# Expert stage of a two-layer decoder trunk: the tokens kept in float32, the gather's split, the slot lists and the register reads moved, and another ending

## The chip, the cores and the metric

The kernel runs on one core of one Trainium2 chip. The metric is the device time of one execution in microseconds (us); the number before the change is the median of three runs. One more execution was recorded by the hardware profiler, and all rows below come from that one. A piece of time under 0.2% (3.8 us) can't be told from no change here.

## What is computed

The reference is a trunk of two layers on 256 tokens of width 1024. Each layer mixes tokens (an attention and a linear attention beside each other), then channels. The change lies in the channel mixing of the second layer, a top-2-of-8 expert SwiGLU with a layer norm behind it:

```python
logits = (x @ router_w).astype(jnp.float32)
top_val, top_idx = lax.top_k(logits, TOP_K)
...
for e in range(N_EXPERTS):
    y = y + gates[..., e:e + 1] * swiglu(x, w_gate[e], w_up[e], w_down[e])
...
x = layer_norm(DN_ALPHA * x + f, ln2_g[layer], ln2_b[layer])
```

Gate and up are 1024 x 3584 per expert, down is 3584 x 1024, everything in float32.

## The kernel before

**Pieces and splits.** All weights come as pieces of 128 x 1024 floats (512 KB) through SP's queue, in one fixed list (`Stream`, L114 to 194): 84 pieces for an expert, 672 in all. A float32 product is made of reduced-precision matmuls: ScalarE rounds a piece to `whi` (L165), VectorE takes the rest `wlo = raw - whi` (L167), and TensorE multiplies the parts. `raw`, `whi` and `wlo` tiles, the gathered tokens and the split tokens all live in one pool of 36 equal slots, tag `k4`. A piece that is marked plain isn't split; TensorE multiplies it in float32, which it records as two matmuls. `caps(raw, spl)` says how many pieces are loaded ahead of the split and split ahead of use in the order in which the program is written: (14, 5) in the expert stage.

**Steps and chunks.** `moe` (L1593) takes the experts by `RANKS`, a sorting by load made on the chip: position 0 is expert 0, the others by rising rank number. Step i computes gate (`mg`) and up (`mu`) of position i in seven chunks of 512 columns, and in the same chunks the down product (`oe`) of position i-1. Even steps are "wide" experts (128 tokens; three matmuls for gate and up: L473 to L475); odd steps are "narrow" ones (64 tokens, both halves of their split tokens in one stationary tile; two matmuls: L1543 and L1544). Down is plain for wide experts (L1557) and split for narrow ones. So an even step has 16 x 3 + 16 matmuls per chunk, an odd one 16 x 2 and 8 float32 products. Step 0 has no down and starts with chunk 1, since `dense` computes expert 0's chunk 0 for all tokens while the router works. After step 7 the down product of the last narrow expert stands alone, first half f=0 of the columns, then f=1, seven chunks each. I call this the last product.

**Chains.** The rest runs in generators that are advanced once per matmul group (`tick`); `lag(n)` lets n ticks pass. `route` (L1259) computes the lists of tokens per expert; its last part is a row of small VectorE instructions that ends with `cnti` (L1360). `gather(i)` (L1375) collects the tokens of the next narrow and the next wide expert by multiplying the tokens with a 0/1 matrix `Pt`: eight blocks of four matmuls (L1394) whose stationary operands are `xnh` and `xnl`, the tokens split once in `route` (L1289 to L1294) and kept in four slots to the end. Gathers 1 to 4 start in chunk 2 of steps 0, 2, 4 and 6; gather 4 has no wide expert, so it takes two slots fewer than gathers 1 to 3. `slots(r)` (L1407) turns the list round: two transposes (L1420) and two products with the gates `gtr` (L1422). It is added at the head of each step. `hidden` and `hidden_t` compute silu(gate) * up and transpose it (L1467, L1481). `scatter` (L1493) multiplies the result of a finished expert (`oh`, `ol`) with the turned list and adds it to `x` (L1511).

**Order.** From behind `dense` on, TensorE, VectorE and ScalarE run as written (`as_written`). SP's loads stand in their list, each waiting for its slot. Expert numbers other than 0 are only known on the chip: SP reads them from `eidi` into registers (L437), at the place where the scheduler put it.

**End.** `overflow` (L1639) reads a count into registers and skips, by a branch (L1649), a loop that isn't needed when no expert has too many tokens. Then `ln_params` loads scale and shift of the last norm, 512 KB each (L1134), and `last_norm` (L1625) computes it.

Of the kernel before, what the change touches and what calls it, by code (L numbers as in the profile page):

```python
# [18 lines left out]
P = 128  # L19
# [94 lines left out]
class Stream:  # L114
# [24 lines left out]
    def dma_to(self, i):  # L139
        while self.n_dma <= min(i, len(self.subs) - 1):  # L140
            src, n, _ = self.subs[self.n_dma]
            if callable(src):
                src = src()
            t = self.k.k4([P, 2, 512], name="raw")
            self.k.nc.sync.dma_start(t[:, :, :n], src[:, :2 * n].rearrange("p (k n) -> p k n", k=2))
            self.raw[self.n_dma] = t
            self.n_dma += 1
# [40 lines left out]
class Kern:  # L188
# [234 lines left out]
    def plan(self):  # L423
# [18 lines left out]
        def add(nm, r, c, j):  # L442
            W.add((nm, r, c, j), [piece(r, i) for i in moe_pieces(nm, c, j)], 512, nm == "md" and self.plain(r))
# [12 lines left out]
    def plain(self, r):  # L456

        return r not in NARROW
# [800 lines left out]
    def route(self):  # L1259
# [20 lines left out]
        self.xn = [[], []]  # L1280
        for t in range(2):
# [7 lines left out]
            hi = self.k4([P, D], F32R, name="xnh")  # L1289
            lo = self.k4([P, D], F32R, name="xnl")  # L1290
            nc.scalar.copy(hi, self.x[t])
            nc.vector.tensor_tensor(lo, self.x[t], f32(hi), op=OP.subtract)
            self.xn[0].append(hi)
            self.xn[1].append(lo)  # L1294
# [80 lines left out]
    def gather(self, i):  # L1375
# [117 lines left out]
    def scatter(self, e, f, oe):  # L1493
# [8 lines left out]
        self.flags.add(("oh", e, f))  # L1502
        yield
# [11 lines left out]
    def down(self, r, c, fs=(0, 1)):  # L1515
# [77 lines left out]
    def moe(self):  # L1593
        nc = self.nc
        self.Pt, self.xe, self.PT, self.ht = {}, {}, {}, {}
        self.taken = False
        self.add_chain(self.route(), ("route",), 1)
        self.dense()
        first = len(self.traced())
        for i, r in enumerate(RANKS):  # L1600
            self.add_chain(self.slots(r), ("slots", r), 1)
            for c in range(0 if i else 1, 7):
                if i % 2 == 0 and c == 2 and i < NE - 1:
# [3 lines left out]
                res = {}  # L1607

# [5 lines left out]
                if i:  # L1614
                    self.run(self.down(RANKS[i - 1], c))
        for f in range(2):
# [5 lines left out]
        g2, b2 = self.ln_params(2, 1, nc.sync)  # L1622
        self.last_norm(g2, b2)

    def last_norm(self, g, b):  # L1625
        nc = self.nc
        mv = [self.norm_stats(t, LN_EPS) for t in range(2)]
        for t in range(2):
            x = self.x[t]
            nb = self.small([P, 1], "nb", 2)  # L1630
            nc.vector.scalar_tensor_tensor(nb, mv[t][:, 0:1], -1.0, mv[t][:, 3:4], op0=OP.mult, op1=OP.mult)
            for h in range(2):
                s = slice(h * 512, (h + 1) * 512)
                nc.scalar.activation(x[:, s], x[:, s], AF.Identity, bias=nb, scale=mv[t][:, 3:4])
                nc.vector.tensor_tensor(x[:, s], x[:, s], g[:, s], op=OP.mult)  # L1635
                (nc.vector if h else nc.gpsimd).tensor_tensor(x[:, s], x[:, s], b[:, s], op=OP.add)  # L1636
                nc.sync.dma_start(self.out[0, t * P:(t + 1) * P, s], x[:, s])

    def overflow(self):  # L1639
# [3 lines left out]
        n = nc.values_load(self.cnti[0:1, 0:1], min_val=0, max_val=S)  # L1643
# [5 lines left out]
        with tc.If(n > 0):  # L1649
            with tc.For_i(0, NE, 1) as e:  # L1650
# [16 lines left out]
                for d in range(8):  # L1667
                    ps = self.bg("xe")
                    for j in range(2):
                        for t in range(2):  # L1670
                            nc.tensor.matmul(ps[:, :P], lhsT=f32(self.xn[j][t])[:, d * P:(d + 1) * P], rhs=p2[:, t],
                                             start=(j == 0 and t == 0), stop=(j == 1 and t == 1))
# [44 lines left out]
    def build(self):  # L1717
# [9 lines left out]
        self.CAP_MOE = (14, 5)  # L1727
        self.LAG = 9
# [56 lines left out]
```

## Time and profile before

| | us |
|---|---|
| median of 3 runs (1896.32 to 1897.02) | 1896.44 |
| the profiled execution | 1896.58 |
| its span in the trace | 1894.8 |
| step 0 (expert 0, chunk 1) starts | 981.49 |
| steps 1, 2, 3 start | 1059.98, 1166.60, 1280.28 |
| steps 4, 5, 6, 7 start | 1392.26, 1504.90, 1616.96, 1729.32 |
| the last product starts and ends | 1837.76, 1875.03 |

The page gives TensorE as busy for 97% of the span, VectorE 77%, ScalarE 61%. Its slices show that the DMA engines are almost full from slice 21 on (about 995 us), which is the expert stage, and only 30% to 60% busy before. So the two halves of the program have different limits, and the shares of the whole span say little about either. A TensorE matmul of 512 columns shows a duration of 0.39 us, but the next one starts 0.23 us after it; starts, not durations, tell the pace.

### The profile page before, as it was taken

The page shows a single profiled execution, that of the slowest core. Times are in us where ns is not written, and L with a number is a line of the kernel's source. Part 1 is how long each engine was busy: PE and PEld are TensorE (multiplying, and loading weights), DVE is VectorE, ACT ScalarE, POOL GpSimd, SP SyncE. Part 2 cuts the span into 40 slices and gives each one's busy share as a digit, 9 for nine tenths or more (in the row PEclk, how much of TensorE's full clock was granted, in tenths as well). Part 3 has the DMA queues.
Part 4 walks back from the last instruction along what each step waited for, and adds up shares of the span by engine and source line. Part 5 has one row for each costly group of instructions (what it writes and reads, how often), then busy time and mean ns, then how long its engine had stood idle before and what let it go on. Part 6 is the DMA issues. An engine that isn't in the chain of part 4 may idle for free. (4 is left out here: it accounts for less than half of the span.)

```text
span 1894.8 us, 27869 instructions
## 1 busy us (share of the span) xinstructions
PE 1844.7 (97%) x9279; PEld 1466.0 (77%) x9279; DVE 1459.6 (77%) x2147; ACT 1164.2 (61%) x1710; POOL 163.0 (9%) x221
## 2 busy tenths in 40 slices
PE   8999999999999999999999999999999999999995
PEld 7998888888889998888878766886678766787663
DVE  7888666675556887757588878998788977989777
ACT  6664555454444754545357767786678866787673
POOL 2113202000001212201220000000000000000000
PEclk9999999999999999999999999999999999999997
DMA  9445343674655445444749999999999999999992
GB/s 322 140 147 179 134 150 115 203 242 147 196 200 191 142 137 189 135 147 145 252 159 335 384 409 408 366 395 391 410 400 365 402 394 409 396 372 409 409 409 107
DMA packets 154374, 513.50 MB, mean 271 GB/s; under 512 B 26320, under 2 KB 28592, under 8 KB 154224
## 3 DMA queue, kind: packets, MB, share of 16 engines
q1 hardware_dynamic: 151984, 504.10, 72.1%
q0 software_dynamic: 2240, 7.56, 1.2%
q8 instruction: 75, 1.23, 0.3%
q14 instruction: 75, 0.61, 0.1%
HBM read 506.09 MB, written 5.51 MB: 270 GB/s over the span
## 5 line engine op out<-in xcount | busy, mean ns | idle before, releaser
L167 DVE TENSOR_TENSOR wlo<-raw,whi 128x1024 fp32r<-128x1024 f32 (+1 forms) x838 | 997.3, 1215 | 219.2 <-ACT whi L165 175.2
L165 ACT CAST whi<-raw 128x1024 fp32r<-128x1024 f32 x838 | 849.7, 1047 | 238.0 <-PE oe L1557 63.6
L1557 PE MATMUL oe<-raw,htp 128*128 128x512 f32 x448 | 197.5, 592 | 0.0
L1557 PEld LDWEIGHTS oe<-raw,htp 128*128 128x128 f32 x448 | 84.7, 190 | 94.6 <-issue 91.9
L627 PE MATMUL qb<-xhl,whi 128*128 128x256 f32 x384 | 110.4, 288 | 0.0
L632 PE MATMUL qb<-xhl,wlo 128*128 128x256 f32 x384 | 108.9, 283 | 0.6 <-DVE wlo L167 0.6
L630 PE MATMUL qb<-xhl,whi 128*128 128x256 f32 x384 | 108.5, 283 | 0.0
L473 PE MATMUL at<-whi,xhl 128*128 128x512 f32 x256 | 106.8, 417 | 0.0
L475 PE MATMUL at<-whi,xhl 128*128 128x512 f32 x256 | 101.2, 395 | 0.0
L474 PE MATMUL at<-wlo,xhl 128*128 128x512 f32 x256 | 100.8, 394 | 0.0
L1543 PE MATMUL mg<-whi,xen 128*128 128x512 f32 x224 | 97.4, 435 | 0.0
L1115 POOL TENSOR_TENSOR bnmv<-bnmv,mhalf 128x1 f32<-128x1 f32 x8 | 7.0, 871 | 1006.6 <-DVE bnmv L1114 1006.6
L1543 PE MATMUL mu<-whi,xen 128*128 128x512 f32 x224 | 91.5, 409 | 0.0
L1544 PE MATMUL oe<-wlo,htn 128*128 128x512 f32 x224 | 89.6, 400 | 0.9 <-DVE wlo L167 0.9
L1543 PE MATMUL oe<-whi,htn 128*128 128x512 f32 x224 | 89.6, 400 | 0.0
L1544 PE MATMUL mu<-wlo,xen 128*128 128x512 f32 x224 | 88.7, 396 | 0.0
L1544 PE MATMUL mg<-wlo,xen 128*128 128x512 f32 x224 | 87.8, 392 | 0.0
L473 PE MATMUL mg<-whi,xe 128*128 128x512 f32 x216 | 87.7, 406 | 0.0
L475 PE MATMUL mg<-whi,xe 128*128 128x512 f32 x216 | 85.2, 394 | 0.0
L473 PE MATMUL mu<-whi,xe 128*128 128x512 f32 x216 | 85.1, 394 | 0.0
L474 PE MATMUL mg<-wlo,xe 128*128 128x512 f32 x216 | 84.9, 393 | 0.0
L475 PE MATMUL mu<-whi,xe 128*128 128x512 f32 x216 | 84.3, 390 | 0.0
(456 smaller groups left out, 3817.5 us busy)
## 6 DMA issues: line engine op xcount, KB each, us to landing
raw<-in_moe SPq DMA_DIRECT2D x672, 512.0 KB
raw<-in_trunk SPq DMA_DIRECT2D x270, 512.0 KB
lx<-LT SPq DMA_DIRECT2D x8, 256.0 KB
Dm<-dx SPq DMA_DIRECT2D x8, 256.0 KB
raw<-in_trunk SPq DMA_DIRECT2D x8, 256.0 KB
lng<-in_ln_g POOLq DMA_DIRECT2D x3, 512.0 KB, 5.8
lnb<-in_ln_b POOLq DMA_DIRECT2D x3, 512.0 KB, 8.0
dx<-zero POOLq DMA_DIRECT2D x4, 256.0 KB, 5.0
```

The costliest lines, as they stand in the source:

```text
L165: k.last_act = nc.scalar.copy(hi[:, :, :n], raw[:, :, :n])
L167: ins = (nc.gpsimd if share and a else nc.vector).tensor_tensor(lo[:, a:b, :n], r[:, :, :n], f32(hi)[:, a:b, :n], op=OP.subtract)
L473: nc.tensor.matmul(o, lhsT=xh, rhs=hi[:, kk, :n], start=st, stop=False)
L474: nc.tensor.matmul(o, lhsT=xh, rhs=lo[:, kk, :n], start=False, stop=False)
L475: mm = nc.tensor.matmul(o, lhsT=xl, rhs=hi[:, kk, :n], start=False, stop=en)
L627: nc.tensor.matmul(o, lhsT=hi[:, kk, w], rhs=self.xhl[k // 2][:, k % 2, :S], start=(k == 0 and b % 2 == 0), stop=False, skip_group_check=True)
L630: nc.tensor.matmul(o, lhsT=hi[:, kk, w], rhs=self.xhl[k // 2][:, k % 2, S:], start=False, stop=False, skip_group_check=True)
L632: self.dense_pe = nc.tensor.matmul(o, lhsT=lo[:, kk, w], rhs=self.xhl[k // 2][:, k % 2, :S], start=False, stop=(k == 7), skip_group_check= ...
L1115: nc.gpsimd.tensor_tensor(mv[:, 3:4], mv[:, 2:3], self.mhalf[:, 0:1], op=OP.pow)
L1543: nc.tensor.matmul(o, lhsT=x(k0 + kk), rhs=hi[:, kk], start=first and i == 0 and kk == 0, stop=False)
L1544: nc.tensor.matmul(o, lhsT=x(k0 + kk), rhs=lo[:, kk], start=False, stop=last and end)
L1557: nc.tensor.matmul(o, lhsT=x(k0 + kk), rhs=w[:, kk], start=first and i == 0 and kk == 0, stop=last and end)
```

## The change

- `route` no longer splits the tokens. It copies them in float32 into two slots `xs` (before: four slots), and each of the eight blocks of each gather splits its own 128 x 256 part into `xsh` (ScalarE) and `xsl` (VectorE) right before its matmuls. These small tiles use buffers of the layer's convolution.
- `slots(r)` is added in chunk 3 of a step and not in front of its first chunk.
- SP reads an expert's number behind the load that precedes its first use; the count for the branch, behind the last load.
- Scale and shift of the last norm are loaded before the expert stage as 4 x 256 rows, split in two parts, and spread over the partitions by eight matmuls at the end. `last_norm` takes its statistics for tokens 128 to 255 on ScalarE.
- In the last product f=1, chunks 3 to 6 are plain float32 pieces. `caps` is (8, 5) from chunk 6 of step 7 on and (6, 8) in the last product. The scatter of f=0 lags six ticks more.

```diff
             if callable(src):
-                src = src()
+                with self.k.behind(self.last_dma):
+                    src = src()
...
-    def plain(self, r):
-        return r not in NARROW
+    def plain(self, r, c=0, f=0):
+        return r not in NARROW or (r == RANKS[-1] and f == 1 and c > 2)
...
-        self.xn = [[], []]
+        self.xs = [self.k4([P, 2, 512], name="xs") for _ in range(2)]
...
-            hi = self.k4([P, D], F32R, name="xnh")
-            lo = self.k4([P, D], F32R, name="xnl")
-            nc.scalar.copy(hi, self.x[t])
-            nc.vector.tensor_tensor(lo, self.x[t], f32(hi), op=OP.subtract)
...
+            for h in range(2):
+                nc.scalar.copy(self.xs[h][:, t], self.x[t][:, h * 512:(h + 1) * 512])
...
         for d in range(8):
             yield from self.take()
+            x = self.xs[d // 4][:, :, d % 4 * P:(d % 4 + 1) * P]
+            xp = [self.mp.tile([P, S], F32R, name=nm, tag=tag, bufs=3).rearrange("p (t c) -> p t c", t=2)
+                  for nm, tag in (("xsh", "cth"), ("xsl", "cy"))]
+            nc.scalar.copy(xp[0], x)
+            nc.vector.tensor_tensor(xp[1], x, f32(xp[0]), op=OP.subtract)
             ps = self.bg("xe")
             for j in range(2):
                 for t in range(2):
-                    nc.tensor.matmul(ps[:, j * n:(j + 1) * n], lhsT=self.xn[j][t][:, d * P:(d + 1) * P],
+                    nc.tensor.matmul(ps[:, j * n:(j + 1) * n], lhsT=xp[j][:, t],
...
         self.flags.add(("oh", e, f))
+        if e == RANKS[-1] and f == 0:
+            yield from self.lag(6)
...
-            if r in NARROW:
+            if r in NARROW and self.plain(r, c, f):
+                yield from self.unsplit(keys, self.oe[f], lambda k: f32(ht)[:, k], **ends)
+            elif r in NARROW:
...
-            self.add_chain(self.slots(r), ("slots", r), 1)
             for c in range(0 if i else 1, 7):
+                if c == 3:
+                    self.add_chain(self.slots(r), ("slots", r), 1)
...
+                if (i, c) == (NE - 1, 6):
+                    self.W.caps(*self.CAP_END[0])
...
+        self.W.caps(*self.CAP_END[1])
         for f in range(2):
             for c in range(7):
                 self.run(self.down(RANKS[-1], c, (f,)))
...
-        g2, b2 = self.ln_params(2, 1, nc.sync)
-        self.last_norm(g2, b2)
+        first = len(self.traced())
+        self.last_norm()
+        self.as_written(first)
...
+    def last_norm(self):
+        nc = self.nc
+        sc = [self.acc("lng") for _ in range(2)] + [self.acc("lnb") for _ in range(2)]
+        for r in range(8):
+            nc.tensor.matmul(sc[r // 2][:, r % 2 * S:(r % 2 + 1) * S],
+                             lhsT=self.sel[:, r % 4:r % 4 + 1].to_broadcast([64, P]), rhs=self.rows[r // 4], start=True,
+                             stop=True)
...
+            nc.scalar.activation(junk, x[:, s], AF.Identity, accum_out=st[:, 0, h:h + 1])
+        mv = self.norm_stats(0, LN_EPS)
+        def scaled(t, h):
+            x = self.x[t][:, h_[h]]
+            nc.vector.scalar_tensor_tensor(x, x, (mv if t == 0 else nm)[:, 0:1], sc[h], op0=OP.subtract, op1=OP.mult)
+        def shifted(t, h):
+            x = self.x[t][:, h_[h]]
+            nc.vector.scalar_tensor_tensor(x, x, mv[:, 3:4] if t == 0 else nm[:, 3:4], sc[2 + h], op0=OP.mult, op1=OP.add)
+            nc.sync.dma_start(self.out[0, t * P:(t + 1) * P, h_[h]], x)
+        scaled(0, 0)
+        scaled(0, 1)
...
+            nc.scalar.activation(junk, x[:, s], AF.Square, bias=nm[:, 1:2], accum_out=st[:, 1, h:h + 1])
+        shifted(0, 0)
+        shifted(0, 1)
...
+        nc.gpsimd.tensor_tensor(nm[:, 3:4], nm[:, 2:3], self.mhalf[:, 0:1], op=OP.pow)
+        for f in (scaled, shifted):
...
+        with self.behind(self.W.last_dma):
+            n = nc.values_load(self.cnti[0:1, 0:1], min_val=0, max_val=S)
...
+        self.CAP_END = ((8, 5), (6, 8))
```

TensorE at the head of expert 0's chunk 1, first before and then with the change (`mg` is the gate product, `PT` the list that is turned round):

```order
L473 MATMUL mg<-whi,xe 128x512
L474 MATMUL mg<-wlo,xe 128x512
L475 MATMUL mg<-whi,xe 128x512
L1420 MATMUL PT<-ident,Pt 128x128 x2
L1422 MATMUL PT<-gtr,Pt 128x8 x2
```

```order
L476 MATMUL mg<-whi,xe 128x512
L477 MATMUL mg<-wlo,xe 128x512
L478 MATMUL mg<-whi,xe 128x512
L476 MATMUL mg<-whi,xe 128x512
L477 MATMUL mg<-wlo,xe 128x512
```

The two products with `gtr` have left this place; they stand two chunks later now.

VectorE in gather 2 with the change (`xsl` is the token's rest, `wlo` a weight's); before, no row of the gather stood here, only the `wlo` rows:

```order
L1395 TENSOR_TENSOR xsl<-xs,xsh 128x256
L169 TENSOR_TENSOR wlo<-raw,whi 128x1024 x4
L1395 TENSOR_TENSOR xsl<-xs,xsh 128x256
L169 TENSOR_TENSOR wlo<-raw,whi 128x1024 x3
L1472 TENSOR_TENSOR mgs<-mgs,mu 128x512
```

Each block's subtraction stands behind the weight splits that were written before it, and its matmuls follow at once on TensorE.

SP's queue where the expert loads begin, before and with the change:

```order
L145 DMA raw<-in_trunk 128x1024 x27
L145 DMA raw<-in_moe 128x1024 x26
L437 TENSOR_LOAD eidi
L437 ISA x2
```

```order
L147 DMA raw<-in_trunk 128x1024 x27
L147 DMA raw<-in_moe 128x1024 x56
L439 TENSOR_LOAD eidi
L439 ISA x2
```

The first register read has moved behind all 56 loads of expert 0; before, six reads stood together behind the 26th.

## Rows read from the trace of the kernel before

**Rows 1.** The page, busy time of an engine, share, instructions.

```profile
PE 1844.7 (97%) x9279; PEld 1466.0 (77%) x9279; DVE 1459.6 (77%) x2147; ACT 1164.2 (61%) x1710; POOL 163.0 (9%) x221
```

**Rows 2.** Stretches: PE, PEld, DVE, ACT, POOL busy, PEclk, DMA share, GB/s.

```profile
985.00:991.00 6.00, 5.74 (x28) 4.96 (x28) 5.83 (x12) 3.25 (x4) 0.00 (x0) 0.72 0.45 160
...
1060.00:1166.00 106.00, 103.17 (x369) 65.40 (x368) 81.16 (x84) 70.55 (x86) 0.00 (x0) 1.00 1.02 408
...
1280.00:1392.00 112.00, 107.82 (x379) 68.27 (x379) 87.75 (x93) 73.20 (x89) 0.00 (x0) 0.98 1.02 402
...
1505.00:1617.00 112.00, 107.83 (x380) 68.05 (x378) 87.67 (x93) 72.96 (x88) 0.00 (x0) 0.98 1.02 403
1617.00:1729.00 112.00, 111.77 (x523) 92.20 (x522) 104.16 (x101) 91.81 (x109) 0.00 (x0) 1.00 1.00 388
1729.00:1838.00 109.00, 107.58 (x388) 68.21 (x387) 86.97 (x95) 72.37 (x90) 0.00 (x0) 1.00 1.03 409
...
1838.00:1875.00 37.00, 32.20 (x121) 24.09 (x121) 32.49 (x33) 23.29 (x26) 0.00 (x0) 0.91 0.46 183
```

**Rows 3.** Timeline 981 to 991 us: start, duration, engine, line, [idle before, releaser].

```profile
981.49 0.39 PE L473 MATMUL mg<-whi,xe 128*128 128x512 f32 x1
...
984.23 0.39 PE L1422 MATMUL PT<-gtr,Pt 128*128 128x8 f32 x2 [1.67 <-DVE gtr L1336]
...
985.50 0.48 PE L473 MATMUL mg<-whi,xe 128*128 128x512 f32 x1
...
986.38 0.15 DVE L1360 CAST cnti<-cnt 128x1 int32<-128x1 f32 x1
...
990.93 0.48 PE L473 MATMUL mg<-whi,xe 128*128 128x512 f32 x1
```

**Rows 4.** Waits of SP's queue, 960 to 1075 us: total, times, longest.

```profile
SPq L437 <- DVE rkr L1336: 7.1, 1, 7.1
```

**Rows 5.** Waits inside step 5, 1535 to 1617 us, engines and SP's queue.

```profile
PEld ht L1481 <- DVE mgs L1467: 3.4, 4, 1.0
...
SPq L145 <- PE oe L1557: 21.5, 10, 4.0
```

**Rows 6.** Waits of SP's queue inside step 7, 1746 to 1835 us.

```profile
SPq L145 <- PE oe L1557: 6.6, 5, 2.0
```

**Rows 7.** Lines of ScalarE, 1200 to 1260 us: busy, mean ns | idle before.

```profile
L1403 ACT CAST xe<-xe 128x256 fp32r<-128x256 f32 x8 | 3.1, 382 | 0.8 <-PE mg L475 0.8
```

**Rows 8.** Lines of VectorE, 1060 to 1190 us.

```profile
L1490 DVE TENSOR_TENSOR htn<-ht,htn 128x256 fp32r<-128x256 f32 x7 | 2.9, 409 | 0.0
```

**Rows 9.** Timeline of step 2 around 1217 us, where gather 2 runs.

```profile
1216.69 2.36 DVE L167 TENSOR_TENSOR wlo<-raw,whi 128x1024 fp32r<-128x1024 f32 x2 [0.64 <-ACT whi L165]
1216.75 0.40 PE L1544 MATMUL oe<-wlo,htn 128*128 128x512 f32 x1
...
1216.98 0.39 PE L1543 MATMUL oe<-whi,htn 128*128 128x512 f32 x1
```

**Rows 10.** Timelines: eight float32 records in step 3; then the last product.

```profile
1292.90 3.60 PE L1557 MATMUL oe<-raw,htp 128*128 128x512 f32 x8
...
1837.76 0.50 PE L1543 MATMUL oe<-whi,htn 128*128 128x512 f32 x1
...
1863.77 0.80 PE L1508 MATMUL sc<-ol,PT 128*128 128x512 f32 x1 [3.93 <-DVE ol L1501]
...
1875.03 0.39 PE L1544 MATMUL oe<-wlo,htn 128*128 128x512 f32 x1
```

**Rows 11.** The end: timeline from 1878 us, and TensorE's branch (ns).

```profile
1882.40 2.93 ACT L1634 ACTIVATE x<-x,nb,bnmv 128x512 f32<-128x512 f32 x4 [6.25 <-DVE nb L1631]
...
1885.56 1.29 DVE L1635 TENSOR_TENSOR x<-x,lng 128x512 f32<-128x512 f32 x2 [2.32 <-DMA lng<-in_ln_g]
...
1888.73 3.15 SPq L1637 DMA_DIRECT2D out_x<-x  x4
...
L1649 PEldq COMPARE_BRANCH  x1: 3795/3795/3795, 1877.6 to 1877.6; - x1
```

More of the change, by code (lines that the diff above doesn't have):

```diff
@@ L142, in dma_to @@
             if callable(src):
-                src = src()
+                with self.k.behind(self.last_dma):
+                    src = src()
             t = self.k.k4([P, 2, 512], name="raw")
-            self.k.nc.sync.dma_start(t[:, :, :n], src[:, :2 * n].rearrange("p (k n) -> p k n", k=2))
+            self.last_dma = self.k.nc.sync.dma_start(t[:, :, :n], src[:, :2 * n].rearrange("p (k n) -> p k n", k=2))
             self.raw[self.n_dma] = t
@@ L442, in add @@
         def add(nm, r, c, j):
-            W.add((nm, r, c, j), [piece(r, i) for i in moe_pieces(nm, c, j)], 512, nm == "md" and self.plain(r))
+            W.add((nm, r, c, j), [piece(r, i) for i in moe_pieces(nm, c, j)], 512, nm == "md" and self.plain(r, c, j))
         for i, r in enumerate(RANKS):
@@ L1596, in moe @@
         self.taken = False
+        self.norm_rows()
         self.add_chain(self.route(), ("route",), 1)
@@ L1621, in moe, with norm_rows @@
         self.overflow()
-        g2, b2 = self.ln_params(2, 1, nc.sync)
-        self.last_norm(g2, b2)
-    def last_norm(self, g, b):
+        first = len(self.traced())
+        self.last_norm()
+        self.as_written(first)
+    def norm_rows(self):
         nc = self.nc
[L1627 to L1631, printed above, removed]
-            for h in range(2):
[L1633 to L1637, printed above, removed]
+        H = 64
+        self.sel = self.small([H, 4], "lnsel", 1, F32R)
+        nc.vector.tensor_tensor(self.sel, self.ident[:H, :4], self.ident[:H, 32:36], op=OP.add)
+        self.rows = []
+        for s in "gb":
+            raw = self.mp.tile([P, S], F32, name="lnraw", tag="cth", bufs=3)[:H]
+            row = self.mp.tile([P, S], F32R, name="lnrow", tag="cy", bufs=3)[:H]
+            nc.gpsimd.memset(raw, 0.0)
+            for p in (0, 32):
+                nc.gpsimd.dma_start(raw[p:p + 4], self.A[f"ln2_{s}"][1].rearrange("(r n) -> r n", r=4))
+            nc.scalar.copy(row, raw)
+            nc.vector.tensor_tensor(row[32:], raw[32:], f32(row)[32:], op=OP.subtract)
+            self.rows.append(row)
@@ L1639, in overflow @@
     def overflow(self):
         tc, nc, A = self.tc, self.nc, self.A
-        n = nc.values_load(self.cnti[0:1, 0:1], min_val=0, max_val=S)
+        with self.behind(self.W.last_dma):
+            n = nc.values_load(self.cnti[0:1, 0:1], min_val=0, max_val=S)
         rk = self.small([P, 2, 8], "rk2")
@@ L1668, in overflow @@
                     ps = self.bg("xe")
[L1669 to L1672, printed above, removed]
+                    for t in range(2):
+                        nc.tensor.matmul(ps[:, :P], lhsT=self.xs[d // 4][:, t, d % 4 * P:(d % 4 + 1) * P], rhs=p2[:, t],
+                                         start=(t == 0), stop=(t == 1))
                     nc.vector.tensor_copy(xe[:, d], ps[:, :P])
```

15 lines of the change are left out of this document (13 added, 2 removed).

## The prediction

> **What bounds the kernel now.** I read the page first, then stretches, then waits, then single rows. TensorE is busy for 97% of the span [rows 1]; no other engine comes near. But the change touches only what begins at 981 us, so the stretches say more. I cut them at the starts of the steps, which the table of times gives. An even step such as step 6 holds 111.77 us of TensorE's work in 112.00 us: TensorE alone sets its length. VectorE has 104.16 us in it, 93% [rows 2]. An odd step holds less of TensorE's work: 107.8 in 112.00 us in steps 3 and 5, 103.17 in 106.00 us in step 1, 107.58 in 109.00 us in step 7. What fills the difference is a question of loads. The DMA engines stand at a share of 1.02 to 1.03 and 402 to 409 GB/s in odd steps [rows 2]. A step brings 84 pieces, 44.0 MB, which is 107.7 us at 409 GB/s; a piece is 1.28 us. So an odd step has two bounds close together, and what decides is how many slots hold pieces that are loaded or split ahead. All the rest of the expert stage (its start, the last product, the end) is chains in which TensorE waits.
>
> All sums stand against the profiled execution, 1896.58 us, which is 0.14 above the median of the runs, so they hold for the median as well. A result within 0.2%, 3.8 us, can't be told from no change.
>
> **1. The start of step 0: -3.** TensorE starts on chunk 1 at 981.49, then meets the list's two products with `gtr`, which VectorE has not computed: 1.67 and 0.64 us idle, and it goes on with `mg` at 985.50 [rows 3]. Behind that the clock falls: the granted clock of 985 to 991 is 0.72 [rows 2], after a stretch in which TensorE stood idle; the level there is the 1.2 GHz one in part. With full pace the work from 985.50 to 990.93 [rows 3] would have taken about 0.72 of 5.43 us, 3.9, so 1.5 us go to the clock. Removed: 2.31 idle and 1.5 clock, 3.8. The two transposes and two products are not removed, but stand in chunk 3, when `gtr` is long there. What is late next: VectorE's chain of small instructions runs up to `cnti` at 986.38 [rows 3], and the weight splits for chunk 1 queue behind it, so a part of the idle time may return as a wait for a `wlo`. I take 3 of 3.8. Bounds: -5, if ScalarE's and VectorE's four full-width splits of the tokens in `route`, replaced by four half-width copies on ScalarE, also leave earlier; +1, if the chain is late all the same.
>
> **2. Two slots more: -11.** The token split held four `k4` slots to the end, `xs` holds two. Of 36 slots that gives two more to pieces in all steps; a split piece costs two slots and a raw one one, so the queue gains about one piece of lead, 1.28 us. The trace has this very experiment: gather 4 has no wide expert and holds two slots fewer, so step 7 runs with two more than steps 3 and 5. Step 7 takes 109 us, they take 112 [rows 2]. Inside, the wait of a transpose for `mgs` in step 5 (3.4 us, four times) [rows 5] is not among step 7's waits, and SP's wait for slots that a plain product holds (`oe`) falls from 21.5 us [rows 5] to 6.6 [rows 6]. The granted clock goes from 0.98 to 1.00 with it. So steps 3 and 5 gain 112.4 - 108.4 = 4 us each by the table of times (their mean length against step 7's). Step 1, at 106.6, begins with a stock; I give it 3, since 2.8 us of its 106 are not TensorE's [rows 2]. Step 7 and the even steps gain nothing: there TensorE is full. Sum -11. Bounds: 0, if the transfers are what limits; -15, if step 7 gains too.
>
> By HBM utilization, which the Trainium skill (Perfetto Trace Analysis, Identifying the Most-Contended Engine) wants to be looked at for DMA in place of busy time, 409 GB/s is 114% of the 358 GB/s it gives, near the 120% it calls the practical ceiling of a single core; by that rule the odd steps are the transfers', 107.7 us is the floor of a step, steps 3 and 5 would gain at most 4.7 each and step 1 nothing: -9.4 in place of -11, and 1883 in the sum. The trace agrees as far as that step 7 stands at 108.4, just above that floor, and disagrees in step 1, which took 106.6.
>
> **3. Register reads: 0.** SP waits 7.1 us for `rkr` before its first read [rows 4], with six reads together. Each read now stands behind the load before its first use. TensorE had no wait on a load there: what it lacked was `gtr` [rows 3]. In SP's queue the read now stands between loads that wait for slots anyway. What covers it is the stock of loaded pieces, up to 14. Without that cover the 7.1 us wait would show; that part is in the bounds of the start, not a gain of its own.
>
> **4. The gather's split: +3.** Added: eight blocks in each of gathers 0 to 4, each a ScalarE copy 128x256 (0.38 us by the same form [rows 7]) and a VectorE subtraction (0.41 us by the same form [rows 8]). That is 3.0 and 3.3 us per gather. Removed: the full-width splits in `route`, four instructions. Gathers 1 to 4 begin in the even steps, where VectorE has 104.16 in 112: 107.5 with it, still under 112. The danger is not the sum but the order. The copy, the subtraction and the four matmuls are written together, so TensorE, which runs as written, comes to a block's matmuls and must wait until VectorE has got through the weight splits queued in front (`wlo`, about 1.18 us each: two in 2.36 [rows 9]) and the block's own 0.41. In step 2 TensorE's `oe` matmuls follow at 0.23 us [rows 9] without a gap, so VectorE is ahead of TensorE by what the slots allow. One block late by one `wlo` costs up to 1.2 us, or 1.3 with the transfer of results; 32 blocks would be 42. On the other side the one more piece of lead (part 2) lets VectorE be 1.28 us further ahead, which is just what a block asks. So a block waits nothing as a rule, and a few in each gather wait part of 1.3. I take 3 in all, 0.1 us a block; bounds 0 and 42.
>
> **5. The last product: -2.** It starts at 1837.76 and its last matmul at 1875.03 [rows 10]. At full pace, 0.23 us from start to start [rows 9], its 112 matmuls and six like them of the scatter would take about 27, so 10 are lost; granted clock 0.91, VectorE busy 32.49 of 37 us [rows 2], and 3.93 us in one wait of the scatter for `ol` [rows 10]. The change makes chunks 3 to 6 of f=1 plain: eight pieces with two products each, 16 x 0.86 us = 13.8 (eight records take 3.60 us [rows 10], two records a product, and I allow 0.43 a record without the tail of the last), in place of 32 split matmuls at 0.23, 7.4. TensorE's own work grows by 6.4 to 33.4; VectorE loses eight splits of 1.18 us, 9.4, and ScalarE as many roundings. The lag of six ticks moves the scatter of f=0 off the place where it waits 3.93 us. So between 33.4, all waits gone (-3.9), and the old waits on top of the new work (+6.5). I take -2, about half of what the better end gives, since float32 products need no split and can't wait for VectorE, but their pieces come later. The other caps, (8, 5) and (6, 8), I cost at nothing: the DMA engines are busy for 0.46 of this stretch [rows 2], so there is room in the queue; without it each late piece would cost 1.28 us.
>
> **6. The end: -2.** TensorE's branch takes 3.795 us [rows 11]. Scale and shift are loaded only behind it and VectorE waits 2.32 us for the first until 1885.56; the last output's issue ends at 1891.88 [rows 11]. Now eight matmuls spread them, behind the branch: some 2 us at the low clock, four of 0.43 before the first scaling. Then eight VectorE passes of about 0.65 us (0.645 each by the `lng` row [rows 11]) and small instructions between, with ScalarE's squares beside. That puts the last issue near 1889.5, -2.3. Bounds -4 and -1. The loads of the rows lie far ahead on POOL's queue, beside work of TensorE before the expert stage; POOL is busy for 9% of the span [rows 1]. Without that cover VectorE's 2.32 us wait would stand here as before.
>
> Sum: -3 - 11 + 0 + 3 - 2 - 2 = -15, so **1881.5 us**.
>
> **The rivals.** *The gather's splits stall TensorE (slower).* In 32 blocks of gathers 1 to 4 TensorE waits the queue of VectorE, 1.3 us each: 1881.5 - 3 + 42 = 1920. For: VectorE at 93% in the even steps [rows 2], the `wlo` rows of 2.36 us [rows 9]. Against: no gap in TensorE there now, and one piece more of lead. It decides from 0.57 us a block on: 32 x 0.57 = 18, which eats all other terms. Chance 0.09; partly so, 0.35 us a block, 1890: 0.12. *Transfers hold the odd steps.* The slots then give nothing and 1881.5 + 11 = 1892.5. For: 408 GB/s and a share of 1.02 in odd steps [rows 2]. Against: step 7 is 3 us shorter with two slots more at the same share. Chance 0.17. *The start moves its wait.* The change then doesn't do what it says: VectorE's chain is the wait, only the waiting tile changes; +3, 1884.5, within the range. Forecast with it 0.56; better than 1873 (the last product at its floor, step 7 gaining) 0.06.
>
> **How the numbers follow.** 1881.5 is the likeliest case. The unknowns of parts 2 and 5 give -6 and +6 about it; the rivals with 1890 and 1892.5 must be in, so the range is 1873 to 1895, with 0.06 below and 0.13 above. Faster by over 0.2% means under 1892.6: forecast, better, the partial stall and a third of the transfers' case (the pieces of the sum are uncertain by some us), 0.79. Within: 0.11. Slower: 0.10.
>
> **What would show it.** Right: step 0 without the 1.67 and 0.64 us idle and a granted clock near 1.00 at 985; steps 3 and 5 at 108 to 109 us without the waits for `mgs`, even steps unchanged; the last product at 34 to 36 us; the last issue 2 us earlier against its end. Wrong: even steps longer by waits of the gather's matmuls on `xsl`, or steps 3 and 5 still at 112.

## The result, and the profile after

The changed kernel takes 1886.53 us (median of 5 runs, 1885.61 to 1887.48) against 1896.44: 0.9947 of the time before, with an interval of 0.9936 to 0.9958. That is 9.9 us less, where 15 were forecast. Its profiled execution took 1885.61 us with a span of 1883.8, 11.0 less than the span before. The spans are compared below.

First stretches of the changed kernel, cut at its own events: the dense part's end, chunk 2 of step 0, and steps 1, 2, 3, 5 and 7 (columns as in [rows 2]).

```profile
960.00:987.00 27.00, 24.83 (x124) 19.59 (x123) 19.40 (x53) 19.12 (x34) 4.53 (x3) 0.94 0.51 175
...
1000.00:1018.00 18.00, 15.51 (x68) 12.47 (x67) 16.25 (x20) 13.68 (x21) 0.00 (x0) 0.91 0.86 304
...
1066.00:1170.00 104.00, 103.55 (x371) 65.58 (x370) 81.28 (x85) 70.60 (x88) 0.00 (x0) 1.00 1.02 406
1170.00:1283.00 113.00, 112.41 (x523) 92.43 (x522) 106.25 (x110) 95.10 (x123) 0.00 (x0) 1.00 1.01 393
1283.00:1390.00 107.00, 105.59 (x379) 67.13 (x378) 87.13 (x92) 72.84 (x89) 0.00 (x0) 1.00 1.03 409
...
1504.00:1611.00 107.00, 105.59 (x378) 67.03 (x377) 86.96 (x92) 72.84 (x90) 0.00 (x0) 1.00 1.03 409
...
1723.50:1831.00 107.50, 106.92 (x386) 67.86 (x385) 86.36 (x93) 70.55 (x89) 0.00 (x0) 1.00 1.03 409
```

Steps 3 and 5 went from 112 [rows 2] to 107, with a full clock and 409 GB/s. Step 2 stayed at 113, with VectorE at 106 us. By the starts of the steps, the span divides so:

| stretch | before | after | difference | forecast |
|---|---|---|---|---|
| up to the dense part of expert 0 | 948.53 | 948.92 | +0.4 | 0 |
| from there to step 0 | 32.96 | 37.95 | +5.0 | in part 1 |
| step 0 | 78.49 | 78.76 | +0.3 | -3 (part 1) |
| steps 1, 3, 5, 7 | 106.62, 111.97, 112.06, 108.44 | 103.87, 107.13, 107.13, 107.42 | -13.5 | -11 (part 2) |
| steps 2, 4, 6 | 113.69, 112.64, 112.36 | 113.67, 113.70, 112.42 | +1.1 | +3 (part 4) |
| last product, to the scatter's last matmul | 39.79 | 38.51 | -1.3 | -2 (part 5) |
| from there to the end | 17.26 | 14.36 | -2.9 | -2 (part 6) |

So the loss lies in front of step 1, where a gain was forecast. The stretch before step 0 first, in TensorE's timeline of the changed kernel (start, duration, engine, line, idle before and releaser):

```profile
973.15 0.33 PE L1399 MATMUL xe<-Pt,xsh 128*128 128x128 f32 x2
975.23 0.44 PE L1399 MATMUL xe<-Pt,xsl 128*128 128x128 f32 x2 [1.74 <-DVE xsl L1395]
...
976.72 0.63 PE L478 MATMUL mu<-whi,xhl 128*128 128x512 f32 x1
977.14 0.52 PE L1399 MATMUL xe<-Pt,xsh 128*128 128x128 f32 x2
```

and in VectorE's:

```profile
969.88 1.52 DVE L1395 TENSOR_TENSOR xsl<-xs,xsh 128x256 fp32r<-128x256 f32 x1
971.32 1.78 DVE L169 TENSOR_TENSOR wlo<-raw,whi 128x512 fp32r<-128x512 f32 x1
973.03 0.67 DVE L1591 SCALAR_TENSOR_TENSOR mgd<-mgd,mg 128x512 f32<-128x512 f32 x1
973.62 1.21 DVE L169 TENSOR_TENSOR wlo<-raw,whi 128x1024 fp32r<-128x1024 f32 x1
974.76 0.41 DVE L1395 TENSOR_TENSOR xsl<-xs,xsh 128x256 fp32r<-128x256 f32 x1
975.76 0.43 DVE L1395 TENSOR_TENSOR xsl<-xs,xsh 128x256 fp32r<-128x256 f32 x1 [0.59 <-PE xe L1399]
978.19 0.42 DVE L1395 TENSOR_TENSOR xsl<-xs,xsh 128x256 fp32r<-128x256 f32 x1 [2.00 <-PE xe L1399]
```

TensorE has done the first half of a block's matmuls and waits for `xsl`; VectorE has three other instructions in front of it; and the next `xsl` waits 2.00 us in its turn for TensorE to free the buffer of the one before. From 976.72 on single matmuls start 0.43 us apart instead of 0.23. Gather 0 takes 15.4 us from its first to its last matmul, 8.7 before.

In step 0, chunk 1 lasts 12.68 us instead of 17.75: the waits for `gtr` of [rows 3] are gone. Chunk 2 lasts 17.42 instead of 12.80. VectorE and then TensorE there, in the changed kernel:

```profile
991.84 10.31 DVE L169 TENSOR_TENSOR wlo<-raw,whi 128x1024 fp32r<-128x1024 f32 x9
1002.07 0.48 DVE L1372 TENSOR_SCALAR Pt<-ioL,rkr 128x128 fp32r<-128x128 f32 x2
```

```profile
1002.89 0.49 PE L1399 MATMUL xe<-Pt,xsh 128*128 128x256 f32 x2 [2.49 <-DVE Pt L1372]
...
1003.90 0.55 PE L477 MATMUL mg<-wlo,xe 128*128 128x512 f32 x1
1004.25 0.63 PE L478 MATMUL mg<-whi,xe 128*128 128x512 f32 x1
...
1007.54 0.40 PE L477 MATMUL mg<-wlo,xe 128*128 128x512 f32 x1
```

VectorE leaves its chain of small instructions at 991.8, has nine weight splits to do without a break, and only then makes `Pt`, which the first block of gather 1 needs. TensorE waits 2.49 us, and the clock falls to its lower level until 1007.5.

In the waits inside step 5 of the changed kernel, over the stretch of [rows 5], `ht` no longer waits for `mgs` (3.4 us there), and SP's queue waits 7.4 us for slots that `oe` holds, where it was 21.5. All waits of TensorE in the whole of step 5 (total, times, longest) are now

```profile
PE sc L1515 <- DVE ol L1506: 0.8, 1, 0.8
PE ht L1486 <- DVE mgs L1472: 0.6, 1, 0.6
```

where before the change `ht` alone waited 3.3 us for `mgs`. Neither wait is for a load.

### The profile page after: what moved, and what is told of

The parts are those of the page before. It is cut to its first block, busy times and chain, and to the rows that moved or that the text cites. A ratio compares the mean times of both kernels' runs of the same rounds, so it can differ in the third digit from the quotient of the medians.

```text
span 1883.8 us, 27959 instructions
## 1 busy us (share of the span) xinstructions
PE 1849.0 (98%) x9287; PEld 1465.9 (78%) x9287; DVE 1462.1 (78%) x2181; ACT 1168.4 (62%) x1750; POOL 160.1 (8%) x225
## 5 line engine op out<-in xcount | busy, mean ns | idle before, releaser
L169 DVE TENSOR_TENSOR wlo<-raw,whi 128x1024 fp32r<-128x1024 f32 (+1 forms) x830 | 987.2, 1215 | 192.8 <-ACT whi L167 155.1
L476 PE MATMUL at<-whi,xhl 128*128 128x512 f32 x256 | 106.8, 417 | 0.0
L477 PE MATMUL mu<-wlo,xe 128*128 128x512 f32 x216 | 84.2, 390 | 0.0
L1553 PE MATMUL oe<-wlo,htn 128*128 128x512 f32 x208 | 81.6, 392 | 0.0
```

The lines of the kernel that those rows point to most:

```text
L169: ins = (nc.gpsimd if share and a else nc.vector).tensor_tensor(lo[:, a:b, :n], r[:, :, :n], f32(hi)[:, a:b, :n], op=OP.subtract)
L476: nc.tensor.matmul(o, lhsT=xh, rhs=hi[:, kk, :n], start=st, stop=False)
L477: nc.tensor.matmul(o, lhsT=xh, rhs=lo[:, kk, :n], start=False, stop=False)
L1553: nc.tensor.matmul(o, lhsT=x(k0 + kk), rhs=lo[:, kk], start=False, stop=last and end)
```

## The experiments

All times of a chip are compared by the ratio to the kernel before on the same chip (its single runs lie between 1893 and 1901 us there). Lengths of chunks and steps come from the traces and repeat from run to run within 0.3 us, but for the stretch before step 0.

### Is the move of the turned list a gain?

In the changed kernel, put back; in the kernel before, moved alone:

```diff
         for i, r in enumerate(RANKS):
+            self.add_chain(self.slots(r), ("slots", r), 1)
             for c in range(0 if i else 1, 7):
-                if c == 3:
-                    self.add_chain(self.slots(r), ("slots", r), 1)
```

> The changed kernel, with the turned list back in front of a step's first chunk. Theory: in step 0 VectorE is what is late, behind its chain of small instructions, so the change only moved TensorE's wait from the products with gtr (chunk 1, 17.75 us before, 12.68 now) to the gather's wait for Pt (chunk 2, 12.80 before, 17.42 now). Then this kernel has chunk 1 at 17 to 18 us, chunk 2 at 12.5 to 13, and 1885.5 to 1888 us in all, beside 1886.5. Rival, as in the prediction: the move is worth 3 us by itself, so 1889 to 1890.5 us, with chunk 1 longer by 5 and chunk 2 not shorter by more than 2.

Measured: 0.9927 (0.9913 to 0.9941), 1883.5 us. Chunk 1 takes 19.13 us, chunk 2 12.86, together 32.0 beside 30.1. TensorE's waits there:

```profile
PE PT L1427 <- DVE gtr L1336: 2.3, 2, 1.7
```

The wait for `Pt` is gone, that for `gtr` is back. Chunk 1 is longer than the 17 to 18 us expected (17.75 before the change); why is open. Step 0 is 1.3 us longer than the change's, but steps 2, 4 and 6 are 0.8, 0.8 and 0.5 shorter, most likely because the four matmuls meet the gather when they stand in chunk 3. From step 0 to the scatter's end the trace is 0.8 us shorter than the change's. The rival (3 us longer) falls. The median is some 3 us below the change's and below the 1885.5 to 1888 expected, more than the trace shows; its single runs spread from 1881.9 to 1887.8, the profiled one being at the upper end, so that rest is not explained.

> The kernel before, with nothing but the turned list moved to chunk 3. Theory (the wait only moves): chunks 1 and 2 of step 0 together stay at 30 to 31 us (30.55 before), a wait for Pt of 2 to 3 us appears at the first block of gather 1, and the time is 1895.5 to 1897.5. Rival, as in the prediction: 1893 to 1894, with chunks 1 and 2 together at 27 to 28 us.

Measured: 1.0017 (1.0008 to 1.0026), slower by some 3 us. Chunks 1 and 2 take 12.68 and 15.57, 28.25 together, and the wait has moved as foreseen:

```profile
PE xe L1394 <- DVE Pt L1372: 2.5, 1, 2.5
```

So the wait takes back 2.8 of the 5.1 us that chunk 1 gives. Step 0 gains 1.7, and steps 2, 4 and 6 lose 1.5, 1.4 and 1.1; from step 0 to the scatter's end it is 1.0 us longer. So the sum was neither theory's: the move alone is a small loss, because what it gives in step 0 it takes in three even steps, where it stands amid the gather. The two profiled executions differ by 4.5 us, but 3.4 of them lie ahead of step 0, where the two programs are the same.

The wait is as long as in the changed kernel, but chunk 2 is 1.85 us shorter here. The difference is the clock. These are the stretches behind the wait, first here, then in the changed kernel:

```profile
1000.90:1004.40 3.50, 3.47 (x17) 3.00 (x18) 3.50 (x4) 2.66 (x5) 0.00 (x0) 1.00 1.02 417
```

```profile
1004.00:1007.50 3.50, 3.50 (x10) 2.76 (x9) 3.40 (x5) 2.77 (x5) 0.00 (x0) 0.52 0.74 274
```

The granted clock stays at 1.00 here and is 0.52 there. Why it fell in one and not in the other is not shown.

### What are two slots worth?

```diff
-        self.n4, self.n2 = 36, 16
+        self.n4, self.n2 = 34, 16
```

> The changed kernel with 34 slots in place of 36, so that pieces have as many as before the change. Theory: steps 3 and 5 go back from 107.1 to 111.5 to 112.5 us, step 1 from 103.9 to 106 to 107, and the waits for mgs return; in all 1897 to 1900 us beside 1886.5. Rival (the gain of the odd steps comes from the turned list's or the reads' new place): steps 3 and 5 stay below 108.5, in all 1886 to 1889.

Measured: 1.0068 (1.0055 to 1.0081), 1909.6 us: 23 us more than the change, twice what was expected. Steps 1, 3, 5 take 106.8, 111.0, 111.0 (+2.9, +3.9, +3.8), about as foreseen, and in step 5 TensorE's wait for `mgs` is back, at a granted clock of 1.00:

```profile
1520.50:1631.50 111.00, 106.25 (x379) 67.08 (x378) 87.51 (x93) 72.88 (x89) 0.00 (x0) 1.00 1.03 408
```

```profile
PE ht L1486 <- DVE mgs L1472: 3.8, 6, 1.1
```

But steps 2, 4 and 6 take 117.0, 117.0 and 114.2 (+3.3, +3.3, +1.7). In step 2 TensorE waits, without the slots:

```profile
PE xe L1399 <- DVE xsl L1395: 1.4, 3, 0.8
PE xe L1399 <- DVE Pt L1372: 1.2, 1, 1.2
```

and with them 0.3 and 0.3 in the changed kernel:

```profile
PE xe L1399 <- DVE Pt L1372: 0.3, 1, 0.3
PE xe L1399 <- DVE xsl L1395: 0.3, 1, 0.3
```

So the slots pay twice: some 11 us in steps 1, 3 and 5, and some 8 in the even ones, besides 1 in step 0 and 1 in step 7. Not all of the 8 is the price of the gathers' splits. The kernel of e2 has as few slots for pieces and the list in the same place, but splits no blocks; its steps 2, 4 and 6 take 115.15, 114.09 and 113.42, and it has the same 1.2 us wait for `Pt` in step 2. Against it the splits cost 1.8, 2.9 and 0.7, some 5.5 in all.

### What stretches the dense part?

```diff
+            hi = self.k4([P, D], F32R, name="xnh")
+            lo = self.k4([P, D], F32R, name="xnl")
+            nc.scalar.copy(hi, self.x[t])
+            nc.vector.tensor_tensor(lo, self.x[t], f32(hi), op=OP.subtract)
...
-                    nc.tensor.matmul(ps[:, j * n:(j + 1) * n], lhsT=xp[j][:, t],
+                    nc.tensor.matmul(ps[:, j * n:(j + 1) * n], lhsT=xp[j][:, t] if i else self.xn[j][t][:, d * P:(d + 1) * P],
```

> The changed kernel, except that gather 0 takes tokens that route splits at full width (four more slots, free after gather 0), as the kernel before did; gathers 1 to 4 split their blocks as in the change. Theory: the splits of gather 0, which run beside the dense chunk with one xsl buffer free, cost the 4.8 us by which step 0 starts later (986.87, of which 0.4 lies ahead of them); here step 0 starts at 981.5 to 983, and the time is 1881 to 1883.5. Rival 1: VectorE's chain is as late, and what is saved is waited for at Pt of gather 1: start 982, chunk 2 longer by 4, 1885.5 to 1887. Rival 2: the four slots cost leads, 1887 to 1890.

Measured: 0.9920 (0.9907 to 0.9933), 1882.9 us. From the dense part's start to step 0 it takes 35.2 us (change 38.0, before 33.0), gather 0 itself 10.3 (15.4, 8.7), and from step 0 on the trace is that of the change within 0.1 us a step. So the splits of gather 0 are worth about 2.8 of the 5 us. Rivals 1 and 2 fall: chunk 2 is 17.44 as in the change, not 4 longer. Expected were nearly 5; the rest, 2.2 us, is still to be found.

VectorE's rows above show where to look: an `xsl` of 1.52 us where the others take 0.41, and a `wlo` half of 1.78 behind it. Beside them GpSimd runs its share of the weight splits, in the changed kernel:

```profile
969.32 3.24 POOL L169 TENSOR_TENSOR wlo<-raw,whi 128x512 fp32r<-128x512 f32 x2 [6.12 <-ACT whi L167]
```

So the next edit keeps GpSimd out of the splits of the dense part:

```diff
         self.norm_rows()
+        self.W.share = False
         self.add_chain(self.route(), ("route",), 1)
```

> The changed kernel, but in expert 0's dense part GpSimd no longer takes half of a piece's weight split (four halves of 128x512 less there; VectorE does whole pieces). In the change's trace, the VectorE instructions of gather 0 that are far over their usual length (an xsl of 1.52 us, a half wlo of 1.78) lie beside GpSimd's two halves at 969.32 to 972.56. Theory: the two engines hold each other up, so that the share saves VectorE nothing; here xsl takes 0.4 to 0.45 us in every block, and the stretch from the dense part's start to step 0 takes 35 to 37 us instead of 37.7 to 38. Rival: VectorE's four halves more (0.6 us each, 2.4) make it as late as the long instructions did, 37.5 us or more, and the time stays within 1 us of the change's.

Measured: 0.9919 (0.9905 to 0.9933), 1880.4 us. From the dense part's start to step 0 it takes 34.2 us (change 38.0). VectorE's rows of gather 0 now:

```profile
971.48 0.42 DVE L1395 TENSOR_TENSOR xsl<-xs,xsh 128x256 fp32r<-128x256 f32 x1
972.16 1.22 DVE L169 TENSOR_TENSOR wlo<-raw,whi 128x1024 fp32r<-128x1024 f32 x1 [0.27 <-ACT whi L167]
973.31 0.42 DVE L1395 TENSOR_TENSOR xsl<-xs,xsh 128x256 fp32r<-128x256 f32 x1
```

The stretch is shorter than the 35 to 37 us expected. Every `xsl` takes 0.42 us, and TensorE's waits for `xsl` add up to 0.7 us in three places. A whole `wlo` takes 1.22 us, while a half took 1.78 beside GpSimd. The rival falls: VectorE has more to do and is earlier. But not all of the 3.7 us is the change's loss. 1.0 of it lies ahead of gather 0, in TensorE's idle time at the transposes `tp`, which the kernel before had as well and for which the trace names no releaser. These rows are the kernel before, the change and this run:

```profile
PE tp L283 <- issue: 1.9, 1, 1.9
```

```profile
PE tp L285 <- issue: 1.9, 1, 1.9
```

```profile
PE tp L285 <- issue: 0.9, 1, 0.9
```

So GpSimd's share accounts for some 2.7 of the 5.0 us. Small VectorE instructions met GpSimd before the change too, in the chain of `route`; this cast of two columns takes 0.17 us elsewhere:

```profile
961.88 1.74 POOL L167 TENSOR_TENSOR wlo<-raw,whi 128x512 fp32r<-128x512 f32 x1 [6.15 <-DVE mx L1283]
962.65 0.99 DVE L1285 CAST ix<-mi 128x2 f32<-128x2 uint32 x1
```

In gather 0 itself only `wlo` stood beside GpSimd then, and now there are also the blocks' `xsl`, for which TensorE waits. That these are the reason is argued and not shown: e12 below takes 3.6 us off a dense part whose gather 0 has no `xsl`. Step 0 is 1.6 us shorter as well (77.15), though its wait for `Pt` is the same 2.49 us: here the granted clock stays at 1.00 behind it, and chunk 2 takes 15.80.

### The end

The changed kernel with the kernel before's `ln_params` and `last_norm`, and no `norm_rows`.

> The changed kernel with the ending of the kernel before (scale and shift loaded behind the branch, no rows kept in the convolution's buffers). Theory: from the scatter's last matmul to the end of the span it takes 17.25 us as before instead of 14.32, +2.9 us. The rows no longer hold two of the three buffers that the gather's xsl shares; if that one free buffer is what stretches gather 0 (15.4 us, 8.7 before), gather 0 falls to 9 to 12 us here, and the two together give -2 to +1 us in all. Rival: gather 0 stays at 15 us, since VectorE's weight splits stand in front of the blocks' own; then +2 to +4 in all.

Beside it the change itself, again:

> The changed kernel itself, on the same chip as the next three, as their measure. By its first times 0.9947 of the kernel before; 0.993 to 0.996 here.

Measured: the change 0.9949 (0.9936 to 0.9962), 1887.05 us; with the old end 0.9952 (0.9939 to 0.9965), 1886.9 us. From the scatter's last matmul to the end it takes 16.81 us instead of 14.32, +2.5. Gather 0 takes 11.8 us instead of 13.7 in this pair (15.4 in the change's first trace), and step 0 starts 35.9 us behind the dense part's start instead of 37.7. So the two effects cancel: the rows kept for the end hold two of three buffers that `xsl` uses, which costs gather 0 about 2 us, and the end gives 2.5. No `xsl` waits for TensorE to free a buffer here; in the change's second trace they wait 2.5 us. The rival falls. The change's two traces differ in gather 0 (15.4 and 13.7) by the clock that followed the same wait, as shown at the end.

### The last product

```diff
-        return r not in NARROW or (r == RANKS[-1] and f == 1 and c > 2)
+        return r not in NARROW
...
-        if e == RANKS[-1] and f == 0:
-            yield from self.lag(6)
...
-        self.CAP_END = ((8, 5), (6, 8))
+        self.CAP_END = ((14, 5), (14, 5))
```

> The changed kernel with the last product of the kernel before: all pieces split, caps left at (14, 5), no six ticks more. Theory, as the prediction's term of -2: from the last product's start to the scatter's last matmul 39.8 us as before, instead of 38.5, and +1 to +2 us in all, with VectorE and ScalarE full. Rival: the two more slots already help here, so 36 to 38 us, and 1 to 2 us less than the change.

Measured: 0.9947 (0.9934 to 0.9960), 1885.9 us, and 38.53 us for the last product, as with the float32 pieces (38.51). Stretches of this kernel's last product, and of the change's:

```profile
1831.30:1870.00 38.70, 32.83 (x128) 24.07 (x126) 33.69 (x35) 24.27 (x27) 0.00 (x0) 0.96 0.45 177
```

```profile
1831.00:1869.50 38.50, 37.04 (x127) 23.08 (x126) 24.52 (x27) 16.62 (x19) 0.00 (x0) 1.00 0.48 180
```

The float32 pieces take 9 us from VectorE and 8 from ScalarE and give TensorE 4 us more to do; the scatter's wait goes (it is 3.92 us here). The end comes at the same moment. Neither theory held: with two more slots, the three edits are worth nothing. But e3, which has the three edits and not the slots, also takes 38.50 us, and the two kernels with neither take 39.79 (before) and 39.18 (e2). So the slots alone give the 0.7 to 1.3 us, the edits alone give them too, and both together give no more. What holds all three at 38.5 is not shown.

### The reads

```diff
-                with self.k.behind(self.last_dma):
-                    src = src()
+                src = src()
...
-        with self.behind(self.W.last_dma):
-            n = nc.values_load(self.cnti[0:1, 0:1], min_val=0, max_val=S)
+        n = nc.values_load(self.cnti[0:1, 0:1], min_val=0, max_val=S)
```

> The changed kernel, with SP's reads of the expert numbers and of the count left where the scheduler puts them, as before the change. Theory, as the prediction's term of 0: SP waits some 7 us for its numbers again, but the loaded pieces cover it, and the time is the change's within 1 us. Rival: loads for chunks 1 and 2 of step 0 come later, step 0 takes 2 us or more longer.

Measured: 0.9946 (0.9932 to 0.9959), 1885.7 us. SP waits 8.2 us for `rkr` as in [rows 4]:

```profile
SPq L438 <- DVE rkr L1335: 8.2, 1, 8.2
```

Step 0 takes 78.73 us, with the late reads 78.76. The wait is covered; the read's place is worth nothing.

### Giving VectorE time at the start

```diff
-                if i % 2 == 0 and c == 2 and i < NE - 1:
+                if i % 2 == 0 and c == (2 if i else 3) and i < NE - 1:
```

> The changed kernel with one edit: gather 1 begins in chunk 3 of step 0 and not in chunk 2. Theory: VectorE is the later engine at the start of step 0 and gains on TensorE in every chunk without down pieces, so one chunk later the wait for Pt (2.5 us) and the low clock behind it are gone: chunk 2 at 12 to 13 us in place of 17.4, chunk 3 not over 14, and 3 to 4.5 us less than the change (0.9949 to about 0.993). Rival: VectorE's lag lasts, and the wait stands in chunk 3: same time as the change within 1 us.

Measured: 0.9922 (0.9908 to 0.9936), 1881.4 us. Chunks 1 to 3 take 12.68, 11.34 and 12.58 (change: 12.68, 17.42, 12.50), step 0 74.27 instead of 78.76, and TensorE has no wait in it. The rival falls.

Then this, with e4's gather 0 and the list added in chunk 2 of step 0 and at the head of the other steps:

```diff
-                if c == 3:
+                if c == (0 if i else 2):
                     self.add_chain(self.slots(r), ("slots", r), 1)
```

> The changed kernel with three edits: gather 0 takes tokens split at full width as in e4; gather 1 begins in chunk 3 of step 0, when VectorE has had two chunks to catch up; the turned list is added in chunk 2 of step 0 and in front of the first chunk of all other steps. Theory: -2.8 (dense part, as e4's trace), -4 (chunk 2 of step 0 at 12.5 to 13.5 us, no wait for Pt), -2 (steps 2, 4 and 6, as e1's trace): 9 us under the change, 0.990 of the kernel before, or below. Rival: VectorE is late all the same, and the waits of step 0 go to another tile: not more than 5 us under the change.

Measured: 0.9901 (0.9885 to 0.9917), 1878.2 us, 9 less than the change on the same chip. Step 0 and steps 1 and 2 as stretches:

```profile
984.50:1059.40 74.90, 74.72 (x364) 62.20 (x363) 68.83 (x90) 60.83 (x85) 0.00 (x0) 1.00 0.91 329
1059.40:1163.20 103.80, 103.38 (x371) 65.60 (x370) 81.19 (x85) 71.02 (x87) 0.00 (x0) 1.00 1.02 408
1163.20:1276.00 112.80, 112.54 (x524) 92.85 (x523) 107.02 (x110) 95.13 (x124) 0.00 (x0) 1.00 1.01 397
```

TensorE is full throughout step 0. Steps 2, 4 and 6 take 112.8, 112.9 and 111.9 (change 113.7, 113.7, 112.4). Last, this kernel with GpSimd kept out of the dense part's splits:

> The kernel of e8 with the same edit. Theory: its dense part (35.6 us to step 0) falls to 33.5 to 35, and the ratio to the kernel before to 0.989 to 0.990. Rival: no difference, 0.990 to 0.991; what remains of the dense part is then not the shared splits.

Measured: 0.9880 (0.9865 to 0.9895), 1874.2 us, the lowest of all, 22 us under the kernel before and better than expected. The dense part takes 32.1 us to step 0, where it took 35.6 in e8 and 33.0 before the change; 1.0 us of either difference is the shorter idle time at `tp`, as in e11.

## Why the prediction was right or wrong

**Part 1, the start (-3): wrong in sign, +5.6 to the start of step 1.** Two steps of it failed. The sentence that took 3 of 3.8 us assumed that a wait moved out of TensorE's way is a wait removed. VectorE, not the list's place, was late: its chain ran to `cnti` about 4.9 us after step 0's start in both traces, and the same lateness met TensorE one chunk later, at `Pt`, for 2.49 us and, in this kernel, with the low clock behind it. Chunks 1 and 2 together went from 30.55 to 30.10. Where the clock didn't fall (e2), they went to 28.25, and the three even steps took the gain back. The text named the possibility ("may return as a wait for a `wlo`", and the third rival) but priced it at +3 within the range, and looked for it at the wrong tile. The other failure is an omission: part 4 counted the splits of gather 0 and then put stalls only on gathers 1 to 4, so the dense part had no term. There the blocks' splits met GpSimd's share of the weight splits, a single free buffer and waiting matmuls. Each of three edits takes a part of the 5.0 us away: 2.7 without GpSimd's share (e11, its 3.7 less the 1.0 at `tp`), 2.8 with gather 0 split at full width (e4), about 2 with the rows out of `xsl`'s buffers (e6). They overlap; e4's and e11's together take 4.9 (e12, its 5.9 less the 1.0 at `tp`), which is nearly all of it.

**Part 2, the slots (-11): right, and low.** Steps 1, 3 and 5 gave 2.75, 4.84 and 4.93, with 3, 4 and 4 forecast, and step 7 gave 1.0. The comparison of step 7 with steps 3 and 5 was the right reading of the trace, though the table of times gives a mean of 112.0 for these two and not 112.4, so that it stood for 3.6 a step. e3 shows the mechanism by taking the slots back: 11.6 of the 13.5 us go. Most of the rest goes with the granted clock in steps 3 and 5, which is 0.98 before the change and 1.00 both with it and in e3; why is open. The prediction took step 7's 108.4 as the end, and steps 3 and 5 went past it. They also went past the 107.7 us that 84 pieces take at 409 GB/s: they stand at 107.1, and step 1 at 103.9. TensorE has 105.6 us of work in 107 there and its 1.4 us of waits are all for VectorE, so now TensorE sets the length of odd steps too, with the transfers close behind. The Trainium skill (Perfetto Trace Analysis, Identifying the Most-Contended Engine) has one look at DMA by HBM utilization, which by its 358 GB/s is 114% here. The trace agrees that the DMA engines are full, with a share of 1.03; what it does not show is that they hold these steps.

**Part 3, the reads (0): right.** e10 shows 0.0, with SP's 8.2 us wait in full view.

**Part 4, the gathers (+3): near, and for the reason given.** Steps 2, 4 and 6 lost 1.1 together, and e2 and e1 put even that to the list's place in chunk 3, 0.5 to 1.5 us a step. The splits alone are hidden; e3 shows that only one more piece of lead hides them: without it the same splits cost some 5.5 us in these steps (e3 against e2). The prediction said that they would be balanced by "the one more piece of lead"; it did not say that the slots would then have two jobs.

**Part 5, the last product (-2): size near, cause wrong.** It gave -1.3, but e7 gives the same without any of the three edits, and e3 the same without the slots. The step that failed is the value taken between 33.4 and the old waits, which left out that the slots of part 2 work here too: beside them TensorE's added work (4 us) and VectorE's relief (9 us) leave the end where it was.

**Part 6, the end (-2): right,** -2.9 in the traces, -2.5 by e6 against e5. Only its price elsewhere was missed, since the rows lie where the gather's buffers are. Behind TensorE's branch no wait for a load is left in the changed kernel's trace, where VectorE waited 2.32 us [rows 11].

The slower rival (1.3 us for each of 32 blocks) did not come, since the lead was there; its mechanism is real, as e3's 1.4 us of waits in one step and gather 0's 1.74 us in one block show. The rival of transfers holding the odd steps did not come either. The wrong 8.6 us of part 1 were made up in part by 2.5 too little in part 2, 2 too much in part 4 and 1 in part 6, so that the sum missed by 4 to 5 us only. That closeness is luck: no reason ties these errors together.

## What to carry to other kernels

Before counting a removed wait as a gain, ask which engine was late and whether its instructions are still the same: if they are, the wait comes back, in whole or in part, at the next tile that it makes, and only work moved off that engine, or time given to it, removes it. Work put between an engine and its consumer in program order costs by lead, not by its own length, so the same splits were free in a stretch with one more piece of lead and cost about 2 us a step without. An engine or a buffer that seemed to help for nothing (GpSimd's halves, the convolution's tiles) has to be priced by a run without it, and again when short instructions with a waiting reader come beside it. GpSimd's halves already cost 1 us before the change, if the idle time at `tp` is what they cost there too. And one trace does not give the price of a wait on TensorE: look at the granted clock behind it, in more than one execution.

## What the runs showed of the hardware

The same wait on TensorE can cost little more than its own length or nearly twice that. Behind the 2.49 us for `Pt` in the changed kernel the clock was at its lower level, 1.2 GHz, for some 3 us (granted clock 0.52 from 1004.0 to 1007.5, 512 columns in 0.43 us instead of 0.23), and chunk 2 became 4.6 us longer; behind the same 2.5 us in e2 and e11 the granted clock stayed at 1.00, and chunk 2 took 15.57 and 15.80 instead of 17.42. It is not a matter of the program alone: in the changed kernel's first trace 1.74 us of waiting for `xsl` were followed by the lower level, and in its second trace (e5) 1.72 us at the same place were not.

```profile
976.70:980.10 3.40, 3.40 (x11) 2.83 (x10) 1.91 (x3) 2.29 (x4) 0.00 (x0) 0.50 0.14 51
```

```profile
980.00:983.60 3.60, 3.60 (x21) 3.12 (x21) 2.67 (x4) 3.10 (x6) 0.00 (x0) 1.00 0.27 74
```

Gather 0 took 15.4 us in the one and 13.7 in the other.

VectorE and GpSimd hold each other up. Beside GpSimd's two halves (969.32 to 972.56 in the changed kernel) VectorE's `xsl` took 1.52 us instead of 0.42 and a half `wlo` 1.78 instead of 0.68, GpSimd's own halves took 1.80 and 1.48 instead of 1.29, and without them (e11) no such row is left in gather 0. The Trainium skill (SBUF — State Buffer, Who interferes with whom) says why: the two engines share a pair of ports under an exclusive lock, so that one stands still while the other holds it. The traces agree with that; they show the lengths and not the lock.

The stretch up to the dense part differed by 2.0 us between two traces of the changed kernel (948.92 and 950.88) and by 2.3 between the kernel before (948.53) and e2 (950.85), whose program is the same there; that is as much as many of the edits here are worth. Only the steps' lengths, which repeat, told them apart.
